# The feed-forward up-projection by one level of Strassen, the gated values by way of DRAM to a down stage of their own

## The chip, the cores and the metric

The kernel runs on one core of a Trainium2 chip. The metric is the device time of one execution in microseconds (us). The five engines of the core are TensorE (PE in the rows, and PEld for its weight loads), VectorE (DVE), ScalarE (ACT), GpSimd (POOL) and SyncE (SP), which issues the DMAs. Each engine works through its own instructions in order; semaphores join them.

## The reference

One layer of a hybrid decoder for 1056 tokens, of which 1024 are a prompt and 32 are samples (8 streams of 4). A state-space and an RWKV mixing sub-layer, an attention to a memory, and a feed-forward sub-layer with a causal convolution follow one another; the change touches the last one alone, and the norm ahead of it:

```python
def rmsnorm(x, g):
    xf = x.astype(jnp.float32)
    y = xf * lax.rsqrt(jnp.mean(xf * xf, axis=-1, keepdims=True) + EPS)
    return (y * g.astype(jnp.float32)).astype(x.dtype)

def conv_ffn(h, buf, w_up, conv_w, conv_b, w_down):
    up = h @ w_up                                   # 1024 -> 2 * 2816
    up, new_buf = causal_dwconv(up, buf, conv_w, conv_b)    # width 3
    gate, val = jnp.split(up, 2, axis=-1)
    return (jax.nn.silu(gate) * val) @ w_down, new_buf

    x = x + cross_attn(rmsnorm(x, p["norm_xa_w"]), mem_k, mem_v, p["xa_w_q"], p["xa_w_o"])
    f, ffn_conv_n = conv_ffn(rmsnorm(x, p["norm_ffn_w"]), ffn_conv, ...)
    return x + f, ...
```

## The kernel before

Everything is laid out with the channels in the 128 partitions and the tokens along the free axis. A product in float32 precision is made of three: each operand is split in a rounded high part and the rest (`split`, L142: a cast on ScalarE, L143, and a subtraction on VectorE, L144), and TensorE adds high by high, high by low and low by high into one PSUM bank. Weights come in tiles of 128 x 1024 by SyncE, are split, and wait in two rings, `w_hi` and `w_lo`. A scheduler sets each engine's order from the order of the code and the rings of buffers, so an instruction can move ahead of others that come before it in the code.

The tokens lie in two halves, 512 and 544 columns (the second holds the samples). `phase_e` is the attention's output projection, once for the half of 544 and then for that of 512: eight tiles m, each 24 matmuls a piece (`gemm`, L217; pieces of 272 + 272 and of 512), the addition of x (L1376, into `pt`, which was loaded at L1374), the split of the sum times the norm's gain into `xq` (L147, L148), the sum of squares (L268, L271), and a store to `x2_d`. The root of the mean square (`row_roots`, L246, L229, L233) and its spreading over the partitions (`spread`, L255) come after all eight tiles. Nobody waits for them there: the root `rbf` is multiplied in later, as `up` evicts its banks (L1464, L1461).

The feed-forward runs over 22 pairs j of projection tiles. `up` makes one tile of 128 channels for all tokens (L1454: pieces of 512, 272 and 272 columns), convolves it (ScalarE L1440 and L1442 for the middle tap, VectorE L1444 and L1446 for the two others), and takes the silu of the first of the pair (L1494). `up_pair` multiplies the two (L1497) and splits the result into `hh`. Groups of 4, 4, 4, 4, 2 and 4 pairs go to `down_all`, which adds their share of the down product into the residual tiles x2 (L1484, L1486; three pieces of 352 columns) while the next group's first pair is made. The last group (L1542) is done in columns of 400, 400 and 256, with the final norm of one piece beside the next. GpSimd has only small work here: a fill of two columns (L1433) and copies of 2 and 16 columns (L1434, L1467, L1468) per tile, and the power of `inv_root` (L233).

## Time and profile before

| what | value |
| --- | --- |
| median of three runs | 1953.26 us (1951.85 to 1959.46) |
| the profiled execution | 1949.68 us |
| its span, first to last instruction | 1947.9 us |
| outside of the span | 1.8 us |
| TensorE busy | 1870.5 us, 96% of the span |
| VectorE busy | 1198.4 us, 62% |
| ScalarE busy | 714.6 us, 37% |
| GpSimd busy | 128.4 us, 7% |

The share of busy time is an average over the stages. A stage is read by its window (who is busy, at which granted clock of TensorE) and by the chain of waits, which follows back from the last instruction what released each step. Up and down take 1181 to 1886 us of the span, the output projection ahead of them some 1080 to 1167, and the last group with the final norm the rest. The profiled execution is 3.6 us shorter than the median.

### The profile page before, as it was taken

The numbers are of one execution on the slowest core, as the hardware profiler recorded it, in microseconds if no ns is written. First come the engines' busy times: TensorE is split into PE (matmuls) and PEld (weight loads), VectorE is DVE, ScalarE is ACT, GpSimd is POOL, SyncE is SP. The second block draws the span as 40 slices with busy tenths as digits, with TensorE's granted clock in tenths as the row PEclk, the third lists the DMA queues.
The fourth block names the chain that finished last, engine by engine and source line by source line (L and its number), as shares of the span: only waits on it lengthen the run. The fifth ranks groups of instructions, "written<-read, shape, count | busy, mean of one in ns | idle before, by whom it ended". The sixth has DMA issues, their size and how long they took to land.

```text
span 1947.9 us, 34518 instructions
## 1 busy us (share of the span) xinstructions
PE 1870.5 (96%) x14150; PEld 1628.5 (84%) x14150; DVE 1198.4 (62%) x2357; ACT 714.6 (37%) x1256; POOL 128.4 (7%) x316
## 2 busy tenths in 40 slices
PE   6999999989999999999999999999999999999997
PEld 6797788865777667799866988999999999999997
DVE  5657677687686677656745645654655545645566
ACT  4443335445444444335534433322322312312231
POOL 0011111010110110000000001000000000000000
PEclk9999999989999899999999999999999999999999
DMA  7521113053222123365266572112112111121112
GB/s 252 174 68 42 37 46 108 30 169 120 79 55 67 53 66 100 120 230 197 82 231 218 157 235 90 43 34 66 33 44 62 32 51 53 31 67 45 44 52 90
DMA packets 104094, 183.78 MB, mean 94 GB/s; under 512 B 36928, under 2 KB 49536, under 8 KB 103936
## 3 DMA queue, kind: packets, MB, share of 16 engines
q1 hardware_dynamic: 103936, 181.58, 30.6%
q8 instruction: 111, 1.82, 0.4%
q14 instruction: 47, 0.39, 0.1%
HBM read 154.32 MB, written 27.22 MB: 93 GB/s over the span
## 4 chain that ended last, share of the span: by engine, by line
PE 81%; DMA 6%; DVE 5%; ACT 3%; POOL 2%; issue 1%; SPq 0%; POOLq 0%; DVEq 0%; ACTq 0%
PE ps_g L217 21%; PE ps_c L1454 10%; PE ps_g L1454 10%; PE ps_y L217 4%; PE ps_g L1484 4%; PE ps_c L1484 4%; PE ps_y L1454 3%; PE ps_x L1454 3%; PE ps_x L1484 2%; PE ps_y L1484 2%; POOL ir_r L233 1%; PE ps_m L535 1%; PE ps_x L608 1%; DVE w_lo L144 1%; DMA dx<-s 1%
## 5 line engine op out<-in xcount | busy, mean ns | idle before, releaser
L217 PE MATMUL ps_g<-act,w_hi 128*128 128x272 f32 (+1 forms) x1728 | 429.8, 336 | 0.2 <-DVE rv L842 0.2
L143 ACT CAST w_hi<-w_raw 128x1024 fp32r<-128x1024 f32 (+1 forms) x196 | 191.8, 979 | 511.4 <-PE ps_g L217 143.6
L217 PEld LDWEIGHTS ps_g<-act,w_hi 128*128 128x128 f32 x1728 | 293.4, 192 | 38.9 <-issue 11.7
L217 PE MATMUL ps_g<-act,w_lo 128*128 128x272 f32 (+1 forms) x864 | 290.6, 336 | 0.1
L144 DVE TENSOR_TENSOR w_lo<-w_raw,w_hi 128x1024 fp32r<-128x1024 f32 (+1 forms) x196 | 222.9, 1137 | 102.3 <-ACT w_hi L143 98.7
L217 PEld LDWEIGHTS ps_g<-act,w_lo 128*128 128x128 f32 x864 | 165.8, 192 | 18.1 <-issue 5.1
L1454 PE MATMUL ps_g<-xq,w_hi 128*128 128x512 f32 (+1 forms) x704 | 177.2, 340 | 0.0
L1454 PE MATMUL ps_c<-xq,w_hi 128*128 128x512 f32 (+1 forms) x704 | 176.9, 340 | 0.0
L1454 PEld LDWEIGHTS ps_g<-xq,w_hi 128*128 128x128 f32 x704 | 121.8, 188 | 14.3
L1454 PEld LDWEIGHTS ps_c<-xq,w_hi 128*128 128x128 f32 x704 | 121.6, 188 | 14.2
L1454 PE MATMUL ps_g<-xq,w_lo 128*128 128x512 f32 (+1 forms) x352 | 119.6, 340 | 0.0
L1454 PE MATMUL ps_c<-xq,w_lo 128*128 128x512 f32 (+1 forms) x352 | 119.5, 340 | 0.0
L1444 DVE SCALAR_TENSOR_TENSOR fo<-fu,vec,fo 128x1024 f32<-128x1024 f32 (+1 forms) x90 | 113.4, 1260 | 6.9 <-ACT fo L1440 5.3
L217 PE MATMUL ps_g<-xq,w_hi 128*128 128x272 f32 (+1 forms) x336 | 85.7, 340 | 0.0
L1454 PEld LDWEIGHTS ps_c<-xq,w_lo 128*128 128x128 f32 x352 | 66.0, 188 | 7.7
L1454 PEld LDWEIGHTS ps_g<-xq,w_lo 128*128 128x128 f32 x352 | 66.0, 188 | 7.6
L1484 PE MATMUL ps_c<-hh,w_hi 128*128 128x352 f32 x288 | 69.7, 323 | 0.0
L1484 PE MATMUL ps_g<-hh,w_hi 128*128 128x352 f32 x288 | 69.7, 323 | 0.0
L1454 PE MATMUL ps_y<-xq,w_hi 128*128 128x272 f32 x352 | 66.4, 286 | 0.0
L1454 PE MATMUL ps_x<-xq,w_hi 128*128 128x272 f32 x352 | 66.4, 286 | 0.0
L1442 ACT ACTIVATE fo<-fus,vec 128x32 f32<-128x32 f32 x44 | 18.2, 414 | 129.0 <-DVE fus L1461 129.0
L217 PEld LDWEIGHTS ps_g<-xq,w_hi 128*128 128x128 f32 x336 | 57.2, 188 | 9.1 <-issue 3.3
(599 smaller groups left out, 3754.9 us busy)
## 6 DMA issues: line engine op xcount, KB each, us to landing
w_raw<-i_w_in SPq DMA_DIRECT2D x52, 512.0 KB, 3.7
w_raw<-i_w_up SPq DMA_DIRECT2D x44, 512.0 KB, 3.7
w_raw<-i_w_out SPq DMA_DIRECT2D x16, 512.0 KB, 4.3
w_raw<-i_xa_w_q SPq DMA_DIRECT2D x16, 512.0 KB, 3.7
ck<-i_ck SPq DMA_DIRECT2D x16, 512.0 KB, 4.5
ck<-i_cv SPq DMA_DIRECT2D x16, 512.0 KB, 4.2
w_raw<-i_xa_w_o SPq DMA_DIRECT2D x16, 512.0 KB, 4.0
w_raw<-i_w_down SPq DMA_DIRECT2D x32, 256.0 KB, 2.7
```

Source lines behind the costliest of these rows:

```text
L143: S.copy(out=hi, in_=src)
L144: V.tensor_tensor(out=lo, in0=src, in1=hi.bitcast(F32), op=ALU.subtract)
L217: PE.matmul(pt[:, :n], a[:, k], b, start=i == 0, stop=i == 3 * nk - 1)
L233: G.tensor_tensor(out=r[:rows, :n], in0=v[:rows, :n], in1=nhalf[:rows, 0:1].to_broadcast([rows, n]), op=ALU.pow)
L535: PE.matmul(pts[e][:, c * P:c * P + P], BK[hs, 4 * q + c, bkw[e]], KQ[hs, 4 * q + c, :], start=True, stop=True)
L608: PE.matmul(py_[hs, c * 64:c * 64 + 64], EE[hs, c, :], Y[hs, c, :], start=True, stop=True)
L1442: S.activation(out=os_, in_=us_[:, :, 2:6], func=AF.Identity, scale=w3[2], bias=vc("fb", mt))
L1444: V.scalar_tensor_tensor(out=o[:, lo:hi], in0=ub[:, j + lo:j + hi], scalar=w3[j], in1=o[:, lo:hi], op0=ALU.mult, op1=ALU.add)
L1454: PE.matmul(pt[:, :n], a[:, k], xf[k][:, b, lo:lo + n], start=i == 0, stop=i == 3 * KT - 1)
L1484: PE.matmul(pt[:, :NW], a[:, k], hs_[k][:, b, cols], start=i == 0, stop=i == 3 * n - 1)
```

## The change

The residual half is kept as it is (`raw`), and the norm is applied before the product. `phase_e` loses the split; a new `operands` scales the half (L1419), cuts it in two along the channels (k and 4 + k) and along the tokens (`lo` and `hi`, 272 or 256 columns each), and makes the seven operands of one Strassen level from the four quarters: B11, T3, T2, T1, T4, B21 and B22, each split in high and low. `up_quads` makes the seven weights of a pair: the weights of the gate tile (`wg`) and of the value tile (`wu`) are the two rows of the left factor, their halves along the input channels its columns. Four of the seven are sums or differences, made by GpSimd (s1 to s4: L1454, L1455, L1457, L1459). `up_pair` runs the seven products, each over 4 k with 272 and 256 columns (L1527), adds them up in eight banks and three helpers (c1 by ScalarE, L1530; u2 and u3 by VectorE, L1532 and L1534), convolves, gates (L1558) and stores the result in DRAM (`h_d`, L1559). When all 22 pairs are done, `hidden` loads them back (L1584) and splits them, and the down product runs as a stage of its own, in four pieces of 264 columns; the last group too.

```diff
-        def phase_e(h, oa, then=lambda m: None):
...
-                xr = pt_()[:, :width]
...
-                a = xp_tile()
-                split_gain(a[:, 0, :width], a[:, 1, :width], xr, vc("nffn", m))
...
+        def phase_e(h, oa):
...
+                xr = rawp.tile([P, width], F32, name=f"raw{h}", bufs=KT)
+                nc.sync.dma_start(out=xr, in_=x1_d[m, :, off:off + width])
...
+            return raw, row_roots([acc], width, one_d, EPS)
+
+        def operands(h, raw, root):
...
+            def scale(k):
+                for pt, lo, w in rs:
+                    V.scalar_tensor_tensor(out=raw[k][:, lo:lo + w], in0=raw[k][:, lo:lo + w], scalar=vc("nffn", k), in1=pt[:, :w], op0=ALU.mult, op1=ALU.mult)
...
+            for k in range(4):
+                scale(4 + k)
+                V.tensor_tensor(out=hi[k], in0=hi[4 + k], in1=hi[k], op=ALU.subtract)
+                put("T3", k, hi[k])
+                V.tensor_tensor(out=lo[k], in0=lo[k], in1=hi[k], op=ALU.add)
+                put("T2", k, lo[k])
+            for k in range(4):
+                V.tensor_tensor(out=hi[k], in0=hi[4 + k], in1=lo[k], op=ALU.subtract)
+                put("T1", k, hi[k])
+                V.tensor_tensor(out=lo[k], in0=lo[4 + k], in1=lo[k], op=ALU.subtract)
+                put("T4", k, lo[k])
...
+        def up_quads():
...
+                wu = f1.tile([P, KT, P], F32, name="w_raw2", bufs=1)
+                nc.sync.dma_start(out=wu, in_=I["w_up"][FT + j])
+                s1, s2, s3, s4 = (f1.tile([P, 4, P], F32, name="ws", bufs=3) for _ in range(4))
+                for q in range(7):
+                    if q == 1:
+                        G.tensor_tensor(out=s1, in0=wu[:, 0:4], in1=wu[:, 4:8], op=ALU.add)
+                        G.tensor_tensor(out=s2, in0=s1, in1=wg[:, 0:4], op=ALU.subtract)
+                    if q == 2:
+                        G.tensor_tensor(out=s3, in0=wg[:, 0:4], in1=wu[:, 0:4], op=ALU.subtract)
+                    if q == 6:
+                        G.tensor_tensor(out=s4, in0=wg[:, 4:8], in1=s2, op=ALU.subtract)
+                    x = (wg[:, 0:4], s2, s3, wu[:, 4:8], s1, wg[:, 4:8], s4)[q]
...
+            for step_, (name, bank, more) in enumerate((("B11", 0, False), ("T2", 1, False), ("T3", 2, False), ("T4", 2, True), ("T1", 3, False), ("B21", 0, True), ("B22", 3, True))):
+                w = next(quads)
+                for q, X in ((1, X1), (0, X0)):
...
+                    if step_ == 0:
+                        S.copy(out=c1[q], in_=pt[:, :n])
+                    elif step_ == 1:
+                        V.tensor_tensor(out=u2[q], in0=c1[q], in1=pt[:, :n], op=ALU.add)
+                    elif step_ == 2:
+                        V.tensor_tensor(out=u3[q], in0=u2[q], in1=pt[:, :n], op=ALU.add)
+                    elif step_ == 3:
+                        out(1, 0, q, add(u2[q], pt))
...
+            nc.sync.dma_start(out=h_d[j], in_=os_[1])
...
+        def hidden(j):
+
+            o = ff.tile([P, NTOK], F32, name="fo", bufs=4)
+            nc.sync.dma_start(out=o, in_=h_d[j])
```

Three places where the order of instructions moves. The first is VectorE at the border between the two halves of `phase_e`. Before, the last tile's eviction, split and squares stand directly ahead of the first eviction (L1376) and the weight splits of the half of 512:

```order
L1376 TENSOR_TENSOR pt_11974<-pt_11974,ps_g_12007 128x272
L144 TENSOR_TENSOR w_lo_12061<-w_raw_12058,w_hi_12060 128x1024
L148 SCALAR_TENSOR_TENSOR xq_12034<-pt_11974,vec_85,xq_12034 128x544
L271 TENSOR_TENSOR acc_11499<-acc_11499,pt_12037 128x544
L229 TENSOR_SCALAR ir_v_12051<-ps_c_12042 68x8
L1376 TENSOR_TENSOR pt_12056<-pt_12056,ps_y_12064 128x512
L144 TENSOR_TENSOR w_lo_12112<-w_raw_12109,w_hi_12111 128x1024
```

Now (`raw1` and `raw0` are the residual tiles of the halves of 544 and 512, `act` and `xq` hold operands), the 60 instructions of `operands` for the half of 544 stand there, of which these are the last ones:

```order
L144 TENSOR_TENSOR act_12054<-raw1_11769,act_12054 128x272
L144 TENSOR_TENSOR act_12054<-raw1_11834,act_12054 128x272
L144 TENSOR_TENSOR act_12055<-raw1_11899,act_12055 128x272
L144 TENSOR_TENSOR act_12055<-raw1_11964,act_12055 128x272
L1397 TENSOR_TENSOR raw0_12155<-raw0_12155,ps_y_12163 128x512
L144 TENSOR_TENSOR w_lo_12196<-w_raw_12193,w_hi_12195 128x1024
```

The eviction and the weight split have moved behind the whole of `operands`. The same holds at the border to the first pair, with 52 instructions.

The second is VectorE around the end of a pair in the up stage. Before, at a pair's end with a group's down product beside it:

```order
L1464 TENSOR_TENSOR fu_14533<-ps_x_14591,rbf_8712 128x272
L144 TENSOR_TENSOR w_lo_14631<-w_raw_14628,w_hi_14630 128x512
L1444 SCALAR_TENSOR_TENSOR fo_14537<-fu_14533,vec_85,fo_14537 128x1024
L1486 TENSOR_TENSOR act_12409<-ps_g_14634,act_12409 128x352
L1444 SCALAR_TENSOR_TENSOR fo_14537<-fu_14533,vec_85,fo_14537 128x1024
L1486 TENSOR_TENSOR act_12409<-ps_g_14648,act_12409 128x352
L1497 TENSOR_TENSOR fo_14537<-fo_14537,fo_14438 128x1056
```

Now, from the last product's eviction of one pair to u3 of the next (`w_hi` and `w_lo` are the targets of weight splits):

```order
L1512 TENSOR_TENSOR fu_14928<-u20_14946,ps_m_14942 128x256
L144 TENSOR_TENSOR w_hi_15138<-ws_15074,w_hi_15138 128x512
L1551 SCALAR_TENSOR_TENSOR fo_15167<-fu_14928,vec_85,fo_15167 128x1024
L1551 SCALAR_TENSOR_TENSOR fo_15177<-fu_14929,vec_85,fo_15177 128x1024
L1551 SCALAR_TENSOR_TENSOR fo_15167<-fu_14928,vec_85,fo_15167 128x1024
L1552 SCALAR_TENSOR_TENSOR fo_15177<-fus_14931,vec_85,fo_15177 128x32
L1551 SCALAR_TENSOR_TENSOR fo_15177<-fu_14929,vec_85,fo_15177 128x1024
L1552 SCALAR_TENSOR_TENSOR fo_15177<-fus_14931,vec_85,fo_15177 128x32
L144 TENSOR_TENSOR w_hi_15239<-ws_15072,w_hi_15239 128x512
L1558 TENSOR_TENSOR fo_15177<-fo_15177,fo_15167 128x1056
L1532 TENSOR_TENSOR u21_15207<-c11_15205,ps_c_15199 128x272
L1532 TENSOR_TENSOR u20_15206<-c10_15204,ps_y_15198 128x256
```

All four taps and the gating now stand together, between the evictions of a pair's last product and the sums u2, and u3 of the next pair (two rows further) stands behind them.

The third is GpSimd at the same place. Before, it has only fills and copies of a few columns:

```order
L1468 COPY fs_12426<-fus_14435 128x16
L1434 COPY fus_15020<-sst_12427 128x8x2
L1467 COPY fp_12425<-fu_14434 128x2
L1433 MEMSET fu_15019 128x2
L1468 COPY fs_12426<-fus_14534 128x16
```

Now the weight sums stand among them (L1459 is s4 of one pair, L1454, L1455 and L1457 are s1, s2 and s3 of the next):

```order
L1553 COPY fp_12564<-fu_14668 128x2
L1459 TENSOR_TENSOR ws_14815<-w_raw_14808,ws_14813 128x512
L1454 TENSOR_TENSOR ws_15072<-w_raw2_15070 128x512
L1491 MEMSET fu_14928 128x2
L1491 MEMSET fu_14929 128x2
L1492 COPY fus_14931<-sst_12566 128x8x2
L1455 TENSOR_TENSOR ws_15073<-ws_15072,w_raw_15068 128x512
L1457 TENSOR_TENSOR ws_15074<-w_raw_15068,w_raw2_15070 128x512
```

s4 and the next pair's s1 stand one behind the other, ahead of the fills that wait for the taps.

## Rows read from the trace of the kernel before

**Rows 1.** Windows: stretch, length, busy us (count) PE PEld DVE ACT POOL, clock, DMA share, GB/s.

```profile
1168.00:1181.00 13.00, 12.20 (x80) 11.00 (x80) 6.88 (x12) 3.64 (x7) 1.34 (x4) 1.00 0.62 201
1181.00:1886.00 705.00, 705.00 (x4392) 662.32 (x4391) 392.50 (x588) 185.33 (x210) 30.60 (x172) 1.00 0.16 47
```

**Rows 2.** The chain of waits in the up and down stage: start, duration in us, what.

```profile
1325.81 3.88 PE ps_c L1484 x24
1343.16 8.53 PE ps_c L1454 x48
1351.69 2.99 PE ps_x L1454 x24
```

**Rows 3.** The chain of waits near the end, the last group's 256 columns.

```profile
1924.85 1.43 PE ps_x L1542 x12
```

**Rows 4.** The chain of waits at the output projection and the first up tile.

```profile
1079.14 3.05 PE ps_m L1287 x12
1121.26 3.69 PE ps_y L217 x16
1128.77 11.05 PE ps_g L217 x48
1139.82 5.49 PE ps_y L217 x24
1167.29 4.81 PE ps_g L1454 x21
```

**Rows 5.** DMA issues: destination and source, queue, count, size, us to landing.

```profile
act<-x_d SPq DMA_DIRECT2D x8, 528.0 KB, 4.7
x_d<-pt SPq DMA_DIRECT2D x16, 256.0 KB, 2.2
pt<-x_d SPq DMA_DIRECT2D x8, 272.0 KB, 2.9
```

**Rows 6.** Groups by form on DVE: form and count, busy us, mean ns, idle before.

```profile
L1444 DVE SCALAR_TENSOR_TENSOR fo<-fu,vec,fo 128x1024 f32<-128x1024 f32 x86 | 110.4, 1284 | 6.4 <-ACT fo L1440 4.7 <-issue 0.3
L1497 DVE TENSOR_TENSOR fo<-fo 128x1056 f32<-128x1056 f32 x21 | 26.4, 1257 | 0.6
L144 DVE TENSOR_TENSOR w_lo<-w_raw,w_hi 128x512 fp32r<-128x512 f32 x32 | 22.3, 696 | 0.7
L148 DVE SCALAR_TENSOR_TENSOR xq<-pt,vec,xq 128x512 fp32r<-128x512 f32 x16 | 11.4, 747 | 1.1 <-ACT xq L147 1.1
L1464 DVE TENSOR_TENSOR fu<-ps_y,rbf 128x272 f32<-128x272 f32 x22 | 9.7, 442 | 37.0 <-PE ps_y L1454 37.0
```

**Rows 7.** The timeline of DVE: start, us, what; two instructions merged in one row.

```profile
689.73 1.29 DVE L537 TENSOR_TENSOR W<-ps_m,cst 128x512 f32<-128x512 f32 x2 [0.26 <-PE ps_m L535]
```

**Rows 8.** The windows around an early gap of TensorE, columns as in rows 1.

```profile
425.00:431.00 6.00, 0.47 (x1) 0.18 (x1) 5.71 (x19) 2.51 (x7) 0.31 (x1) 0.50 0.59 149
431.00:434.00 3.00, 2.68 (x8) 0.97 (x8) 2.31 (x9) 0.84 (x2) 0.00 (x0) 0.50 0.96 313
```

**Rows 9.** Groups by form on ACT.

```profile
L143 ACT CAST w_hi<-w_raw 128x512 fp32r<-128x512 f32 x32 | 19.9, 621 | 132.6 <-PE ps_x L1484 58.0 <-PE ps_y L1484 57.4 <-PE ps_x L1454 8.6
L1440 ACT ACTIVATE fo<-fu,vec 128x1024 f32<-128x1024 f32 x43 | 53.5, 1244 | 0.0
```

**Rows 10.** The timeline at one tap, and two GpSimd lines' durations (min/median/max in ns).

```profile
1185.02 1.28 DVE L1444 SCALAR_TENSOR_TENSOR fo<-fu,vec,fo 128x1024 f32<-128x1024 f32 x1
1185.26 1.10 POOL L1434 COPY fus<-sst 128x16 f32<-128x16 f32 x1 [2.75 <-DVE fo L1446]
...
L1434 POOL COPY fus<-sst x44: 197/198/1097, 1182.2 to 1862.0; 128x16 f32<-128x16 f32 x44
...
L447 POOL COPY last_u<-ub x28: 178/752/1757, 82.4 to 696.0; 128x1 f32<-128x1 f32 x28
```

**Rows 11.** Groups by form on POOL.

```profile
L474 POOL MEMSET Mt<- 128x1024 f32 x1 | 1.0, 951 | 0.0
L1057 POOL COPY hp<-xcs 128x192 f32<-128x192 f32 x1 | 0.6, 603 | 5.8 <-PE ps_m L785 5.8
```

More of the change, by code (lines that the diff above doesn't have):

```diff
@@ L1471, in hybrid_step @@
-        LAST = ((0, 400), (400, 400), (800, 256))
-        NP = 3
-        NW = NTOK // NP
+        NW = NTOK // 4
+        LAST = tuple((i * NW, NW) for i in range(4))
+        def hidden(j):
+            o = ff.tile([P, NTOK], F32, name="fo", bufs=4)
+            nc.sync.dma_start(out=o, in_=h_d[j])
+            hh = [xp_tile()[:, :, :2 * NW] for _ in range(2)]
+            for i in range(2):
+                split(hh[i][:, 0], hh[i][:, 1], o[:, 2 * NW * i:2 * NW * i + 2 * NW])
+            return hh
```

252 lines of the change are left out of this document (146 added, 106 removed).

## The prediction

> **What bounds the kernel now.** I read the windows first, stage by stage, then the chain of waits for the length of each product, then the groups by form for what stands on the other engines. From 1181 to 1886 us, where up and down alternate, TensorE is busy in all 705 us, at the full granted clock (2.4 GHz); VectorE has 392.5 us of work there and GpSimd 30.6 [rows 1]. No wait ends last in that stage: it is as long as its matmuls, so a multiplication that is left out is worth its whole time there, as long as its operands still come in time. So the prediction has two halves, what the matmuls give back and where TensorE now has to wait.
>
> **What the matmuls give back.** One projection tile is 24 matmuls of 512 and 24 of 272 columns, 8.53 us, and 24 more of 272, 2.99 us [rows 2]: 11.52 us, 44 times, 506.9 us. After, a pair of tiles is seven products, each of 12 matmuls of 272 columns (2.99 / 24 = 124.6 ns) and 12 of 256 (1.43 / 12 = 119.2 ns, [rows 3]): 7 × 12 × 243.8 ns = 20.48 us, 22 times, 450.5 us. That is **−56.4 us**. The down products keep their columns and are cut in four pieces of 264 where there were three of 352. A 352 costs 3.88 / 24 = 161.7 ns [rows 2]; for a 264 I take 122 ns, between the two short ones: 1728 × 122 − 1296 × 161.7 = +1.2 us, and the last group the same way less than that; together I book **+1.1 us**.
>
> **The hand-over into the output projection, +3.7 us.** The residual tiles have a new place in SBUF, over buffers that the last head's matmuls read. Before, x was prefetched while softmax still ran; now its load waits for the matmuls of L1287, which begin at 1079.14 and end by 1082.2 [rows 4]. A load of 272 KB lands after 2.9 us [rows 5], two additions of 0.44 us follow [rows 6], and only then are the banks free: about 1085.9, where TensorE went on at 1082.2.
>
> **Between the two halves of the output projection, +19.5 us.** Normalizing and building the seven operand sets is new on VectorE: per half 28 splits and 16 sums, and scalings on top (16 for the half of 544 columns, 8 for the other). In the order these stand in one piece ahead of the first eviction of the second half and ahead of the split of its third weight tile. Two subtractions of 512 back to back take 1.29 us where one alone takes 0.70, so each gives 0.10 us to the one before [rows 7]. A sum of 272 is then 0.442 − 0.10 = 0.35 us [rows 6], and a scaling, by the 0.05 that it costs more at 512 [rows 6], 0.40: 44 × 0.35 + 16 × 0.40 = 21.8 us. Count from T1 = 1121.26, where the first half's products end [rows 4]. The scale is spread 7.5 us later (1128.77), the operands are done at 29.3, an eviction (0.6) and a weight split (1.2) bring TensorE its next tile at T1+31.1. TensorE meanwhile has two weight tiles ready: the first ends with the roots at T1+7.5, the second (5.49 us, [rows 4]) at 13.0. It is idle for 18 us, and the six tiles that are left end at 31.1 + 6 × 5.49 = 64.0, where before the stage ended at 1167.29, T1+46.0: +18.0. After a gap the clock has to come back: around 431 us TensorE sat nearly idle for 6 us, and the 3 us of matmuls after it still ran at the granted clock of 0.50, which is 1.2 GHz [rows 8]. 3 us at half speed lose 1.5 us: **+19.5 us**.
>
> **Before the first pair, +16.5 us.** The same again for the half of 512. Evicting, squaring, root and spreading took at most 7.5 us above; six are enough here. Then 8 scalings of 512 at 0.65 and 44 of 256 at 0.34: 20.2 us. At T2+27 the first weight that stands behind them is split. TensorE has by then done the products on the half of 544 columns and waits with 90 of 168 matmuls to go, 11 us: pair 0 ends at T2+38.7, not at 20.5, **+18.2**. The stall that stood at the same place before falls away: 0.8 us of 13 idle [rows 1] and some 1.4 us of root matmuls that now lie in the gap, −2.2; a cold clock takes 0 to 1.5 again. I book **+16.5**.
>
> **From up to down, +11.7 us.** The hidden values come back from DRAM. The x2 loads wait for the last products (their tiles were operands), and the first two loads of hidden values stand behind them on SyncE. One of 528 KB lands after 4.7 us [rows 5], a split follows, so TensorE begins some 6.3 us late and works for 4.4 us on the two it has; the third and fourth load stand behind the store of the last pair, which comes 9 us after the last product (below), and the fourth also waits for it to land, 2.2 us by a store of 256 KB [rows 5]: 9 + 2.2 + 4.7 + 0.6 = 16.5. Of that 4.4 + 2.2 us are work: 10 us idle, with the clock **+11.7**. The bound above is 17, if the eight x2 loads in flight slow the others.
>
> **Without anything more** the sum is −56.4 + 1.1 + 3.7 + 19.5 + 16.5 + 11.7 = −3.9 us: 1945.8 against the profiled execution of 1949.68. That execution lies 3.6 us under the median of 1953.26; against the median it is 1949.4.
>
> **Inside the stage: who holds whom.** Per pair VectorE now has some 14.7 us of work in 20.5, but in one lump. Let t = 0 be the end of a pair's last product. Its eviction ends at 0.5, a cast (0.62) and the first tap (1.24) on ScalarE [rows 9] at 2.0; four taps of 1.28 less the overlap, 1.2 each [rows 6], with the sample columns end at 7.2, a weight split (0.6) at 7.8, the gating (1.26 less the overlap, [rows 6]) at 9.0, two sums u2 at 9.7, a split at 10.3, and u3 at 10.65. The product T4 adds into the bank from which u3 reads, so TensorE waits for it. It gets there after six and a bit of the short products: 3 × 2.93 for B11, T2, T3, half of T1 (1.50) and three matmuls, 10.65. There is no slack: what delays VectorE in these 10 us is a stall, 21 times.
>
> GpSimd now makes four weight sums of 512 columns per pair. A GpSimd copy of 16 elements that began under a tap of VectorE took 1.10 us and ended 0.06 us after the tap; the same copy takes 0.20 us as a rule, and one of a single element runs from 178 to 1757 ns [rows 10]. With two inputs in SBUF, VectorE holds GpSimd off. That GpSimd holds VectorE off as long, no row shows: its pieces in before are too short. I take it that it does, since whatever keeps the second out is held by the first. The Trainium skill, "SBUF — State Buffer", section "Who interferes with whom", says the same and more: VectorE with two SBUF inputs and a GpSimd instruction that reads SBUF take the same port pair, whoever comes first has it for the whole instruction, the other is fully blocked. By that rule each sum that gets in costs its whole length; were the lock on GpSimd's side alone, the sum would stay at 1949.
>
> What a sum of 512 takes is bounded by a fill of 1024, 951 ns, so 0.5 us, and by a copy of 192 in 603 ns, so 1.6 [rows 11]; 192 columns there were partly blocked, so I take the middle, 1.0. (The Trainium skill, "GPSIMD Engine Reference", section 3.1, has 4497 ns for an addition of 2048, an estimate of 1.12 here; with it the stall would be 1.7 us a pair instead of 1.5.) The order puts s4 at t = 1.45, released by a split: it ends at 2.45 and the taps begin 0.4 late. s1 of the next pair follows as its load lands, within the taps: 1.0. s2 is released at the split before the gating and mostly runs under the u2 sums, whose input is in PSUM: 0.1. s3 lies later. **1.5 us a pair, 21 times, +31.5 us**; with 0.5 per sum it is 0.5 a pair (+10), with 1.6 it is 2.6 (+55).
>
> **Forecast:** 1945.8 + 31.5 = 1977.3 against the profiled execution, 3.6 more against the median: **1981 us**.
>
> **The rivals.** *GpSimd doesn't stop VectorE* (not slower): its sums fall in the gaps of VectorE, or only GpSimd is held off, as the rows of before literally show. Then 1949, no change. It decides at 0.65 us of stall a pair; below that the time is under 1963. For it: VectorE has 6 us free in each pair. Against: they lie after t = 11, and three of the four sums are released before. *The hand-overs overlap* (faster): if the order of the operands lets TensorE begin the first pair's early products while the later operands are made, and ScalarE's casts hide, half of 19.5 + 16.5 + 11.7 goes, with no stall in the pairs: 1949 − 24 = 1925. Against: the rows of VectorE's order stand in one lump, and a queue runs in order. *The heavy end*: 2.6 a pair, 2004.
>
> **How the numbers follow.** About 0.5%, 10 us, is what a measurement of this kernel can tell from no change, so the bounds are 1943 and 1963. The forecast with its heavy end has 0.58. No stall, or one under 0.65 a pair, 0.27; the hand-overs cheap, 0.15. The range runs from 1941 (no stall, hand-overs 8 us cheaper) to 2004 and leaves out most of the faster case and a little above.
>
> **What would show it.** Right: 20.5 us of matmuls but a pair every 22; TensorE's wait ahead of T4 ended by VectorE's u3; taps of over 1.28 us where a GpSimd sum runs; gaps of 18, 16 and 10 us at the three hand-overs. Wrong: a pair every 20.5 us, taps at their old 1.28; or gaps under 8 us; or GpSimd itself late, with TensorE waiting for a weight split.

## The result: 2.4% slower

The changed kernel takes 2002.51 us (median, 1994.44 to 2003.99), the kernel before 1952.55 us in the same comparison: a ratio of 1.0244, with a 95% interval of 1.0203 to 1.0285. The forecast was 1981 us, slower, with a range of 1941 to 2004; its direction and mechanism came in, and the sum was 21.5 us short.

The profiled execution of the changed kernel took 2003.78 us, with a span of 2002.0 us. Its page begins with the busy times, and its fourth part sums the chain that ended last:

```profile
PE 1846.5 (92%) x15248; PEld 1632.6 (82%) x15248; DVE 1338.2 (67%) x2711; ACT 790.5 (39%) x1541; POOL 287.9 (14%) x405
...
PE 67%; DVE 13%; issue 7%; ACT 5%; DMA 5%; POOL 2%; SPq 0%; POOLq 0%; ACTq 0%; DVEq 0%
```

TensorE's busy time fell by 24 us (1870.5 before), and not by the 56 us that a matmul count gives. In part that is because matmuls that run at a lower granted clock are busy for longer; in part it stands in the pairs, at the full clock: the 21 pairs behind the first are busy for 442.87 us, where the count gives 430.1. The idle time of TensorE doubled, from 77 to 156 us. The windows show where; the first is one pair of the up stage, from just behind the last product of one pair to just behind that of the next, then come four around the passage between the two halves of the output projection (the root, the matmuls after it, the gap, the matmuls after that), the middle of the first pair and the whole of it, the other 21 pairs, and the start of the down products. Columns are as in [rows 1]: length, then busy us (and instructions) of PE, PEld, DVE, ACT and POOL, the granted clock, the DMA share and GB/s.

```profile
1279.37:1302.40 23.03, 21.10 (x170) 20.68 (x169) 17.49 (x28) 9.33 (x17) 8.72 (x12) 1.00 0.21 71
1126.00:1128.00 2.00, 0.24 (x3) 0.01 (x1) 0.00 (x0) 0.00 (x0) 1.64 (x1) 1.00 0.26 100
1130.00:1133.00 3.00, 3.00 (x9) 2.32 (x8) 2.32 (x7) 1.83 (x4) 0.00 (x0) 0.51 0.01 3
1138.00:1154.00 16.00, 0.50 (x3) 0.10 (x1) 14.79 (x41) 9.37 (x25) 0.00 (x0) 0.66 0.00 0
1154.00:1163.00 9.00, 9.00 (x26) 6.78 (x27) 3.47 (x5) 1.48 (x3) 0.00 (x0) 0.65 0.53 177
1197.00:1221.00 24.00, 14.92 (x64) 11.45 (x62) 22.95 (x57) 11.64 (x32) 2.09 (x4) 0.73 0.06 15
1190.28:1233.10 42.82, 31.62 (x182) 27.71 (x182) 32.38 (x75) 16.45 (x43) 8.86 (x14) 0.80 0.13 42
1233.10:1715.21 482.11, 442.87 (x3528) 433.96 (x3527) 364.76 (x565) 196.01 (x356) 176.90 (x248) 1.00 0.21 75
1724.00:1730.00 6.00, 5.82 (x26) 5.79 (x27) 2.64 (x4) 1.83 (x4) 0.00 (x0) 0.50 0.92 294
```

Against [rows 1], where TensorE was busy in every microsecond of the stage, a pair now has 1.93 us in which it stands still. In the 16 us of the gap VectorE works on the operands almost without a break, and TensorE has three matmuls; in the next line TensorE is busy throughout, but at a mean granted clock of 0.65 (0.50 is its lower level, 1.2 GHz). The same stands on a smaller scale at the root: 1.76 us in which TensorE waits, and then 3 us of matmuls at 0.51. In the kernel before, the root passed at the same distance from the first half's end without this:

```profile
1126.00:1128.00 2.00, 2.00 (x9) 1.32 (x8) 0.16 (x1) 0.15 (x1) 1.60 (x1) 1.00 0.55 211
1130.00:1133.00 3.00, 3.00 (x14) 2.44 (x14) 0.16 (x1) 0.00 (x0) 0.00 (x0) 1.00 0.60 202
```

(windows of the kernel before, columns as above; its first half ends within 0.3 us of the same time).

The timeline of TensorE names the waits (start, us, what; in brackets the idle time before and what ended it). The first of these is the hand-over into the output projection, the second the one between its halves, the third is in the first pair, the fourth in an ordinary pair, the last the hand-over to the down products:

```profile
1080.65 0.52 PE L214 MATMUL ps_g<-act,w_hi 128*128 128x272 f32 x2 [3.48 <-DVE raw L1397]
...
1153.93 1.19 PE L214 MATMUL ps_y<-xq,w_hi 128*128 128x512 f32 x2 [15.50 <-DVE raw L1397]
...
1218.90 1.96 PE L1527 MATMUL ps_m<-act,w_hi 128*128 128x272 f32 x7 [3.38 <-DVE w_hi L144]
...
1292.14 1.77 PE L1527 MATMUL ps_x<-xq,w_lo 128*128 128x272 f32 x12 [1.49 <-DVE u L1534]
...
1724.18 0.81 PE L1603 MATMUL ps_g<-xq,w_hi 128*128 128x264 f32 x2 [8.97 <-ACT xq L143]
```

The fourth is the product T4, which waits for VectorE's u3 (L1534), as the prediction had it. It returns with 1.48 to 1.49 us in 19 pairs, and over the whole stage it comes to 30.8 us:

```profile
L1527 PE MATMUL ps_x<-xq,w_lo 128*128 128x272 f32 x264 | 40.3, 303 | 30.8 <-DVE u L1534 30.8
```

Why u3 is late stands on VectorE and GpSimd in that same pair, VectorE's rows first:

```profile
1281.17 5.43 DVE L1551 SCALAR_TENSOR_TENSOR fo<-fu,vec,fo 128x1024 f32<-128x1024 f32 x3 [0.46 <-ACT fo L1548]
...
1286.69 1.27 DVE L1551 SCALAR_TENSOR_TENSOR fo<-fu,vec,fo 128x1024 f32<-128x1024 f32 x1
...
1289.82 0.42 DVE L1532 TENSOR_TENSOR u<-c,ps_c 128x272 f32<-128x272 f32 x1
1290.17 0.41 DVE L1532 TENSOR_TENSOR u<-c,ps_y 128x256 f32<-128x256 f32 x1
1290.50 1.24 DVE L144 TENSOR_TENSOR w_lo<-w_raw,w_lo 128x512 fp32r<-128x512 f32 x1
1291.67 0.42 DVE L1534 TENSOR_TENSOR u<-u,ps_x 128x272 f32<-128x272 f32 x1
...
1280.80 1.29 POOL L1459 TENSOR_TENSOR ws<-w_raw,ws 128x512 f32<-128x512 f32 x1 [2.20 <-DVE w_hi L144]
1282.17 2.16 POOL L1454 TENSOR_TENSOR ws<-w_raw 128x512 f32<-128x512 f32 x1
...
1288.26 1.70 POOL L1492 COPY fus<-sst 128x16 f32<-128x16 f32 x1
1289.92 1.28 POOL L1455 TENSOR_TENSOR ws<-ws,w_raw 128x512 f32<-128x512 f32 x1
```

The sum s4 (L1459) begins 0.37 us ahead of the first tap and ends 0.92 us after the tap's start. s1 (L1454) stands waiting from 1282.17, gets in between two taps, and ends at 1284.33; alone such a sum takes 1.29. The three taps that are merged in the first row end 5.43 us after they began; without GpSimd beside them three take 3.68 us (experiments 1, 4 and 9). A fourth tap without company takes 1.27. s2 (L1455) begins at 1289.92 beside the two u2 sums, which have one input in PSUM and keep their 0.42 us, and then meets the weight split at 1290.50, which has two inputs in SBUF and takes 1.24 instead of 0.69. So 1.75 us and some 0.55 us stand ahead of u3. s2 comes at that place because a copy of 16 columns (L1492) stands ahead of it in GpSimd's order: alone it takes 0.20 us, but here it begins in a split, lasts through the gating (L1558, from 1288.65 to 1289.90) and ends at 1289.96.

Over all pairs, the tap's group (88 instructions, mean 1683 ns) stands against 1284 ns in [rows 6]; s1, which waits among them, stands with 2061 ns:

```profile
L1551 DVE SCALAR_TENSOR_TENSOR fo<-fu,vec,fo 128x1024 f32<-128x1024 f32 x88 | 144.8, 1683 | 10.1 <-ACT fo L1548 10.1
L1454 POOL TENSOR_TENSOR ws<-w_raw 128x512 f32<-128x512 f32 x22 | 45.3, 2061 | 158.0 <-ACT xq L143 156.0 <-DMA w_raw<-i_w_up 0.4
```

**The balance of the two profiled executions**, stage by stage, from where TensorE's stages end (spans of 2002.0 and 1947.9 us):

| stage | after − before, matmul saving set apart | predicted |
| --- | --- | --- |
| all ahead of the output projection (not touched) | −5.0 | 0 |
| first half of the output projection | +5.3 | +3.7 |
| second half, with the gap ahead of it | +22.8 | +19.5 |
| first pair | +20.0 | +16.5 |
| the other 21 pairs, over 20.48 us each | +52.0 | +31.5 |
| down products and final norm | +15.5 | +12.8 |
| up matmuls, by the count | −56.4 | −56.4 |
| sum | +54.2 | +27.6 |

### The profile page after: what moved, and what is told of

The parts are those of the page before. It is cut to its first block, busy times and chain, and to the rows that moved or that the text cites. A ratio compares the mean times of both kernels' runs of the same rounds, so it can differ in the third digit from the quotient of the medians.

```text
span 2002.0 us, 37716 instructions
## 1 busy us (share of the span) xinstructions
PE 1846.5 (92%) x15248; PEld 1632.6 (82%) x15248; DVE 1338.2 (67%) x2711; ACT 790.5 (39%) x1541; POOL 287.9 (14%) x405
## 3 DMA queue, kind: packets, MB, share of 16 engines
q1 hardware_dynamic: 111424, 205.37, 31.5%
## 4 chain that ended last, share of the span: by engine, by line
PE 67%; DVE 13%; issue 7%; ACT 5%; DMA 5%; POOL 2%; SPq 0%; POOLq 0%; ACTq 0%; DVEq 0%
PE ps_g L214 21%; PE ps_m L1527 4%; PE ps_y L214 4%; DVE fo L1551 4%; PE ps_g L1603 3%; PE ps_c L1603 3%; PE ps_g L1527 3%; PE ps_x L1527 2%; PE ps_y L1603 2%; PE ps_c L1527 2%; PE ps_x L1603 2%; ACT fo L1548 1%; POOL ir_r L230 1%; DVE fo L1558 1%; ACT w_hi L143 1%
## 5 line engine op out<-in xcount | busy, mean ns | idle before, releaser
L144 DVE TENSOR_TENSOR w_lo<-w_raw,w_hi 128x1024 fp32r<-128x1024 f32 (+1 forms) x152 | 168.9, 1111 | 77.9 <-ACT w_hi L143 72.5
L1551 DVE SCALAR_TENSOR_TENSOR fo<-fu,vec,fo 128x1024 f32<-128x1024 f32 x88 | 144.8, 1683 | 10.1 <-ACT fo L1548 10.1
L1527 PE MATMUL ps_m<-act,w_hi 128*128 128x272 f32 x528 | 79.9, 294 | 13.2 <-DVE w_hi L144 12.1
L1527 PEld LDWEIGHTS ps_m<-act,w_hi 128*128 128x128 f32 x528 | 70.3, 190 | 18.1 <-DVE w_hi L144 16.9
L1603 PE MATMUL ps_g<-xq,w_hi 128*128 128x264 f32 x392 | 74.5, 287 | 9.0 <-ACT xq L143 9.0
L1527 PE MATMUL ps_m<-xq,w_hi 128*128 128x256 f32 x528 | 74.2, 283 | 0.0
L1527 PE MATMUL ps_c<-xq,w_lo 128*128 128x272 f32 (+1 forms) x528 | 72.4, 286 | 0.0
L1603 PE MATMUL ps_c<-xq,w_hi 128*128 128x264 f32 x380 | 71.9, 286 | 0.0
L1603 PEld LDWEIGHTS ps_g<-xq,w_hi 128*128 128x128 f32 x392 | 61.9, 191 | 9.2 <-ACT xq L143 9.2
L1527 PE MATMUL ps_x<-xq,w_lo 128*128 128x272 f32 x264 | 40.3, 303 | 30.8 <-DVE u L1534 30.8
L1527 PEld LDWEIGHTS ps_m<-xq,w_hi 128*128 128x128 f32 x528 | 68.3, 191 | 0.0
L1527 PEld LDWEIGHTS ps_c<-xq,w_lo 128*128 128x128 f32 x528 | 68.2, 191 | 0.0
L1454 POOL TENSOR_TENSOR ws<-w_raw 128x512 f32<-128x512 f32 x22 | 45.3, 2061 | 158.0 <-ACT xq L143 156.0
L214 PEld LDWEIGHTS ps_g<-xq,w_hi 128*128 128x128 f32 x336 | 59.2, 194 | 10.1 <-issue 3.3
```

The lines of the kernel that those rows point to most:

```text
L144: V.tensor_tensor(out=lo, in0=src, in1=hi.bitcast(F32), op=ALU.subtract)
L214: PE.matmul(pt[:, :n], a[:, k], b, start=i == 0, stop=i == 3 * nk - 1)
L1454: G.tensor_tensor(out=s1, in0=wu[:, 0:4], in1=wu[:, 4:8], op=ALU.add)
L1527: PE.matmul(pt[:, :n], w[:, a], X[name][k][:, b], start=i == 0 and not more, stop=i == 11, skip_group_check=True)
L1551: V.scalar_tensor_tensor(out=o[:, 0:2 * T], in0=ub[i][:, t:t + 2 * T], scalar=w3[t], in1=o[:, 0:2 * T], op0=ALU.mult, op1=ALU.add)
L1603: PE.matmul(pt[:, :NW], a[:, k], x[:, b], start=i == 0, stop=i == 3 * n - 1)
```

## The experiments

The theory to be tested: what makes a pair longer is GpSimd's *reading* of SBUF during VectorE's taps and splits, and u3 has no slack, so that each delay goes into the time whole. The rival: the pair is longer for another reason (VectorE's larger load as such, the order of the products, the loads), and the stretched taps only go along with it.

**1. Without the four weight sums.** The products get the unsummed weight halves in their place, so four of seven products are not those of the reference; all else stays.

```diff
-                        G.tensor_tensor(out=s1, in0=wu[:, 0:4], in1=wu[:, 4:8], op=ALU.add)
-                        G.tensor_tensor(out=s2, in0=s1, in1=wg[:, 0:4], op=ALU.subtract)
...
-                        G.tensor_tensor(out=s3, in0=wg[:, 0:4], in1=wu[:, 0:4], op=ALU.subtract)
...
-                        G.tensor_tensor(out=s4, in0=wg[:, 4:8], in1=s2, op=ALU.subtract)
```

> GpSimd's four weight sums of a pair are left out (the products take the unsummed weights in their place, so the output is not the reference's); all else stands. In the changed kernel a pair takes 23.03 us, of which 7 x 2.94 = 20.6 are products. If GpSimd's sums hold VectorE's two-input instructions off (the lock), the taps go back to 1.28 us, u3 comes in time, no gap stands ahead of T4 and a pair takes 20.6 us: 21 x 2.45 = 51 us less, about 1951 us. If VectorE's lump of work is too late by itself, or the weight splits are, the gap of 1.49 us stays in most part and a pair takes over 22 us: 1980 or more.

Measured: 1951.19 us, ratio to before 1.0005 [0.9971, 1.0038]. The groups of VectorE's taps and of TensorE's first T4 product:

```profile
L1543 DVE SCALAR_TENSOR_TENSOR fo<-fu,vec,fo 128x1024 f32<-128x1024 f32 x88 | 109.0, 1280 | 12.0 <-ACT fo L1540 12.0
...
L1519 PE MATMUL ps_x<-xq,w_lo 128*128 128x272 f32 x264 | 39.4, 299 | 0.4 <-DVE u L1526 0.4
```

The taps have their old 1280 ns, and TensorE's wait for u3 has gone from 30.8 us in all to 0.4. A pair takes 20.72 us. So the sums cost 2.31 us a pair (23.03 − 20.72), and some 50 us in all, as much as the whole loss. This shows that they are the cause, not yet how.

**2. The sums on VectorE.** The same four sums, 0.69 us each there, `V` for `G`:

```diff
-                        G.tensor_tensor(out=s1, in0=wu[:, 0:4], in1=wu[:, 4:8], op=ALU.add)
+                        V.tensor_tensor(out=s1, in0=wu[:, 0:4], in1=wu[:, 4:8], op=ALU.add)
```

> The same four sums, on VectorE in place of GpSimd. VectorE gets 4 x 0.6 = 2.4 us more a pair (some 17 of 20.6), s4 ahead of the taps, where it fits into the wait for ScalarE, and the three others behind u3. By the lock nothing but the work itself is left: taps of 1.28 us, u3 at most 0.2 us late, a pair of 20.6 to 21.0 us, 1951 to 1960 us. If the amount of work on VectorE were the cause, this is the worst place for the sums: over 23 us a pair, 2002 or more.

Measured: 1952.55 us, ratio 1.0016 [0.9996, 1.0036]; a pair takes 20.71 to 20.72 us, a tap 1278 ns:

```profile
L1551 DVE SCALAR_TENSOR_TENSOR fo<-fu,vec,fo 128x1024 f32<-128x1024 f32 x88 | 108.9, 1278 | 0.5 <-ACT fo L1548 0.5
```

VectorE does more work than in the changed kernel, and the pair is as short as without the sums. VectorE's load as such is therefore not what makes the pair long, and the rival loses its first form.

**3. The operands of the first half queued behind the evictions of the second.** `operands` is cut into 20 steps, and some of them are placed behind the eviction of each tile of the second half, so that TensorE's banks come free sooner:

```diff
+        def some(m, ev):
+            with tc.issue_after(ev.ins):
+                for _ in range((3, 3, 3, 3, 2, 2, 2, 2)[m]):
+                    next(ops1, None)
+        raw0, root0 = phase_e(0, oa0, some)
```

> Only the operands of the half of 544 columns move: VectorE's 60 instructions are queued two or three steps behind each eviction of the half of 512, not in one piece ahead of the first. If that lump is what makes TensorE idle for 15.5 us at the border and lets the clock fall behind it, the second half of the output projection ends some 48 us after the first, not 68.8: 20 us less, about 1982 us. If VectorE has no room for it there (2.6 us of own work and some 2.7 of operands in a tile of 5.49 us), tiles are stretched and under 10 us are won.

Measured: 1993.21 us, ratio 1.0219 [1.018, 1.0258]. Against the changed kernel this is 9 us, where 20 were expected. In the trace the gap of 15.50 us is gone, and two smaller ones stand at the third tile, one of 0.94 us and this one:

```profile
1151.86 0.53 PE L214 MATMUL ps_g<-xq,w_lo 128*128 128x512 f32 x1 [2.87 <-DVE w_lo L144]
```

The second half of the output projection ends at 1175.15 instead of 1190.28 us, with all ahead of it 0.4 us later: 15.6 us gained there, some 5 fewer than expected. Three steps ahead of the third tile's weight split were too many; the split (L144) had to wait for them. The rest of the shortfall in the median does not show in this trace, which is 15.1 us shorter than that of the changed kernel (1988.69 against 2003.78); two of the four executions took 1998 us and left no trace. A pair still takes 23.03 us. So the gap between the halves was a matter of order, as the prediction said, and a cost of its own beside the pairs.

**4. The same sums on GpSimd, but later.** A GpSimd copy of one column that reads u3 stands ahead of s4, and s1 to s3 follow it; so the four sums run after u3, and not beside the taps.

```diff
+                        with (tc.issue_after(behind[-1]) if behind else ExitStack()):
+                            G.tensor_tensor(out=s1, in0=wu[:, 0:4], in1=wu[:, 4:8], op=ALU.add)
...
+                        tk = f1.tile([P, 1], F32, name="tk", bufs=2)
+                        t_ = G.tensor_copy(out=tk, in_=u3s[-1][:, 0:1])
+                        with tc.issue_after(t_.ins):
+                            behind.append(G.tensor_tensor(out=s4, in0=wg[:, 4:8], in1=s2, op=ALU.subtract).ins)
```

> The four sums stay on GpSimd with all their work, and are only held back: s4 of a pair and with it s1, s2 and s3 of the next wait for u3 of that pair, so they run while VectorE has gaps. By the lock the taps are 1.28 us again, u3 is in time, and a pair takes 20.6 to 21 us: 1951 to 1960 us, as with no sums at all. If the sums cost by their work or by bandwidth, wherever they stand, nothing is won; if the weights are now late, TensorE waits for a weight split ahead of B22 or of the next pair's T2 instead.

Measured: 1953.37 us, ratio 0.9999 [0.9958, 1.004]. From the timeline, VectorE's taps of one pair and the split behind u3, then GpSimd's first two sums of that pair:

```profile
1294.12 3.68 DVE L1558 SCALAR_TENSOR_TENSOR fo<-fu,vec,fo 128x1024 f32<-128x1024 f32 x3 [0.45 <-ACT fo L1555]
...
1305.25 1.11 DVE L144 TENSOR_TENSOR w_hi<-ws,w_hi 128x512 fp32r<-128x512 f32 x1 [1.85 <-ACT w_hi L143]
...
1303.25 1.31 POOL L1465 TENSOR_TENSOR ws<-w_raw,ws 128x512 f32<-128x512 f32 x1
1304.52 1.30 POOL L1457 TENSOR_TENSOR ws<-w_raw 128x512 f32<-128x512 f32 x1
```

Nothing is left out, no sum is shorter, and a pair takes 20.71 us. The sums still hold VectorE off: the split at 1305.25 takes 1.11 instead of 0.69 us. But there no product waits for VectorE. So it is the place of the sums that costs, and a collision of the same kind costs nothing 10 us later.

**5. All together.** Late sums, the interleaved operands with a lighter start (2, 2, 1, 1, 1, 1, 2, 2), and the first three hidden values loaded in tiles of their own while the last pairs still run:

```diff
+                for _ in range((2, 2, 1, 1, 1, 1, 2, 2)[m]):
+                    next(ops1, None)
...
+            if j == FT - 3:
+                for i in range(3):
+                    o = ff.tile([P, NTOK], F32, name="fh", bufs=3)
+                    nc.sync.dma_start(out=o, in_=h_d[i])
+                    first.append(o)
```

> Three edits together: the late sums, the operands of the half of 544 queued behind the evictions of the half of 512 (with a more even share per tile than the first try, whose third tile waited 3.8 us), and the hidden values of the first three pairs loaded back during the up stage. Late sums alone gave 1953 us. The border should give 18 us (15.5 by the trace of the first try, and most of its 3.8), the border to down 7 of its 8.4: 1953 - 25 = 1928 us, 1.1% under the kernel before. If the borders' gaps only move on to the next wait (the roots, the first pair's operands, the loads of x2), 1940 or more.

Measured: 1930.12 us, ratio 0.9927 [0.9901, 0.9952]: faster than before, as expected. TensorE's up stage is again without a hole, seven products for eight:

```profile
1240.00:1600.00 360.00, 360.00 (x2921) 358.43 (x2921) 275.78 (x473) 158.89 (x296) 160.45 (x224) 1.00 0.22 81
```

The second half of the output projection ends at 1169.7 us and the gap to the down products is 2.76 us, where 8.97 stood. A new wait stands at the border to the first pair. VectorE works on the leftover operands of the half of 544 columns (first row, six splits in one), while GpSimd's power for the root waits beside them and with it TensorE's spreading of the scale:

```profile
1175.81 2.19 DVE L144 TENSOR_TENSOR act<-raw,act 128x272 fp32r<-128x272 f32 x6
...
1174.91 3.96 POOL L230 TENSOR_TENSOR ir_r<-ir_v,nhalf 128x4 f32<-128x4 f32 x1 [12.10 <-DVE ir_v L226]
...
1178.93 1.12 PE L252 MATMUL ps_c<-ident,ir_r 128*128 128x128 f32 x4 [4.47 <-POOL ir_r L230]
```

**6. Fills in place of the sums.** Each sum is replaced by two GpSimd fills, one of the sum's tile (512 elements) and one of a scratch tile (904), which only write; the products are not those of the reference.

```diff
-                        G.tensor_tensor(out=s1, in0=wu[:, 0:4], in1=wu[:, 4:8], op=ALU.add)
-                        G.tensor_tensor(out=s2, in0=s1, in1=wg[:, 0:4], op=ALU.subtract)
+                        G.memset(s1[:, 0:4], 0.25); G.memset(scr, 0.0)
+                        G.memset(s2[:, 0:4], 0.25); G.memset(scr, 0.0)
```

> In place of each of GpSimd's sums stand two fills, of 512 and 904 columns, which only write, and take about as long (some 1.3 us); the weights are wrong by that, so the output is not the reference's. If the lock is on what GpSimd reads, as the Trainium skill says (SBUF - State Buffer, Who interferes with whom), the taps are 1.28 us, a pair is 20.7 and the time 1951. If any GpSimd work of that length there stops VectorE, the taps stay near 1.7 us, a pair is over 22 and the time 1985 or more.

Measured: 1950.1 us, ratio 1.0008 [0.999, 1.0025]; a tap takes 1280 ns. That would speak for the theory, but the trace takes the verdict away: the 88 scratch fills depend on nothing, and the scheduler placed them ahead of the stage, from 1076 to 1158 us. In the pairs only the short fills stood:

```profile
1079.34 0.85 POOL L1460 MEMSET scr<- 128x904 f32 x1
...
1281.47 0.53 POOL L1458 MEMSET ws<- 128x512 f32 x1 [2.10 <-DVE w_hi L144]
```

0.53 us for 1.28 is no equal burden. Inconclusive, and repeated in experiment 9.

**7. s1 twice.** One more sum among the taps:

```diff
+                        G.tensor_tensor(out=s1, in0=wu[:, 0:4], in1=wu[:, 4:8], op=ALU.add)
```

> GpSimd makes s1 twice, one right after the other, all else as in the changed kernel. If each sum that gets in costs VectorE its whole length, the second gets in at the next border between two taps and costs 1.2 us more a pair, 21 times: 26 us, about 2028. If what is lost is a fixed wait per pair (one turn of the lock), 2002 stays.

Measured: 2022.62 us, ratio 1.0395 [1.0357, 1.0432], 20 us over the changed kernel where 26 were expected. The taps and the two sums of one pair:

```profile
1282.60 6.47 DVE L1552 SCALAR_TENSOR_TENSOR fo<-fu,vec,fo 128x1024 f32<-128x1024 f32 x3 [0.45 <-ACT fo L1549]
...
1283.60 2.16 POOL L1454 TENSOR_TENSOR ws<-w_raw 128x512 f32<-128x512 f32 x1
1285.83 2.15 POOL L1455 TENSOR_TENSOR ws<-w_raw 128x512 f32<-128x512 f32 x1
```

The three taps take 6.47 instead of 5.43 us, and a pair 24.07 instead of 23.03: 1.04 us in both. What the taps lose goes into the pair one for one, which is the second half of the theory. The sum itself costs less than its length of 1.28 us (the expectation took 1.2); the traces don't show where the rest goes.

The changed kernel holds a smaller dose as well. At the taps ahead of its last pair s4 stands alone, since no further pair needs an s1 and an s2:

```profile
1695.68 4.39 DVE L1551 SCALAR_TENSOR_TENSOR fo<-fu,vec,fo 128x1024 f32<-128x1024 f32 x3 [0.45 <-ACT fo L1548]
...
1695.31 1.29 POOL L1459 TENSOR_TENSOR ws<-w_raw,ws 128x512 f32<-128x512 f32 x1 [2.20 <-DVE w_hi L144]
```

The split ahead of u3 keeps its 0.68 us there, and the last pair takes 21.42 us, 0.70 over a pair without sums (20.72). With none, one, two and three sums beside them, three taps thus take 3.68, 4.39, 5.43 and 6.47 us: s4 costs 0.71, and each sum that waits and gets in 1.04.

**8. Late sums and the early loads of hidden values**, without the interleaving: the edits of experiment 4 and the last piece of the diff of experiment 5.

> The late sums, and the hidden values of the first three pairs loaded back during the up stage into tiles of their own. If the gap of 7.7 us at the border to down is the wait for these loads and for the last pair's store, it shrinks to 1 or 2 us: 6 to 7 less than the late sums alone, about 1946. If the x2 loads or the splits end it, it stays above 5.

Measured: 1943.64 us, ratio 0.9974 [0.9951, 0.9998]. The gap ahead of the down products is 1.27 us:

```profile
1674.19 0.51 PE L1617 MATMUL ps_g<-xq,w_hi 128*128 128x264 f32 x2 [1.27 <-ACT xq L143]
```

Against experiment 4, where this gap was 7.74 us, that is 9.7 us less: 6.5 of gap, and most of the rest is what the clock lost there behind it (a granted clock of 0.56 over the first 6 us of down products there, which is 2.6 us, and of 1.00 here). Against experiment 5 it leaves 13.5 us for the interleaving, where the trace of experiment 3 had 15.6.

**9. Long fills, held in place.** As experiment 6, but the scratch fill is placed right behind the fill of the sum's tile, so that both stand where the sum stood:

```diff
+            def fill(t):
+                with tc.issue_after(G.memset(t, 0.25).ins):
+                    G.memset(ff.tile([P, 904], F32, name="scr", bufs=1), 0.0)
...
+                        fill(s1)
+                        fill(s2)
```

> In the run before, the longer of the two fills was moved out of the up stage by the scheduler, so only fills of 0.53 us stood there. Now each of GpSimd's sums is a fill of 512 columns with one of 904 held right behind it, some 1.4 us, so that the first tap, and the split behind the gating, run beside a fill; the weights are wrong by that, so the output is not the reference's. If only what GpSimd reads collides with VectorE's two-input instructions (the Trainium skill, SBUF - State Buffer, Who interferes with whom), the taps stay at 1.28 us, a pair at 20.7 and the time at about 1950. If fills hold VectorE off as well, the taps come to 1.5 us or more on average, a pair to over 21.5 and the time to 1970 or more.

Measured: 1951.44 us, ratio 0.9996 [0.996, 1.0033]; a pair takes 20.71 us. One pair's fills and VectorE's taps, and the tap's group:

```profile
1283.40 0.53 POOL L1448 MEMSET ws<- 128x512 f32 x1 [2.18 <-DVE w_hi L144]
1283.87 0.85 POOL L1449 MEMSET scr<- 128x904 f32 x1
...
1283.80 3.68 DVE L1555 SCALAR_TENSOR_TENSOR fo<-fu,vec,fo 128x1024 f32<-128x1024 f32 x3 [0.45 <-ACT fo L1552]
```

```profile
L1555 DVE SCALAR_TENSOR_TENSOR fo<-fu,vec,fo 128x1024 f32<-128x1024 f32 x88 | 109.1, 1281 | 10.0 <-ACT fo L1552 10.0
```

GpSimd is at work for about as long as one sum, and the first tap runs beside it from 1283.80 to the end of the fill at 1284.72. Those 0.92 us are as long as the first tap ran beside s4 in the changed kernel, where it cost 0.71 us; here no tap is longer. The fills in place of s2 stand beside the split ahead of u3, which keeps its 0.68 us; the others lie later. So it is not GpSimd's being busy that stops VectorE; what a sum does and a fill doesn't is to read SBUF (and to add, see below). The Trainium skill, "SBUF — State Buffer", section "Who interferes with whom", says just this: a VectorE instruction with two SBUF inputs contends with a GpSimd instruction that reads SBUF, and not with one that only writes. Runs 1, 4 and 9 agree with it, and so does the u2 sum, with one input in PSUM, that kept its 0.42 us beside s2.

**10. Experiment 5 with the leftover operands later.** The last steps of the half of 544 columns (T1 and T4 in part, B21, B22) are queued behind the first operands of the half of 512, so that VectorE is free when the root is due:

```diff
+                for _ in range((2, 2, 1, 1, 1, 1, 2, 0)[m]):
...
+        ops0 = operands(0, raw0, root0)
+        for _ in range(8):
+            t2 = next(ops0)
+        with tc.issue_after(t2.ins):
+            for _ in ops1:
+                pass
+        for _ in ops0:
+            pass
```

> The three edits together, and what was left of the operands of the half of 544 (its last T1 and T4, and B21 and B22, which the first pair needs last) moved behind the first operands of the half of 512. In the three edits the power on GpSimd took 3.96 us and not 1.03, beside a row of splits on VectorE that stood there. If that was the lock, on the chain to the first pair, it takes 1.03 again and the first pair is ready about 3 us earlier: 1927 us against 1930. If the operands as a whole set the first pair's end, whatever their order, the power is short again and the time stays.

Measured: 1928.66 us, ratio 0.9863 [0.981, 0.9915]. The power takes 1.02 us again, and TensorE's spreading comes 4.4 us earlier than in experiment 5 (2.9 us, counted from the end of the first half); but the gap has moved to a weight split behind the operands, which comes as late as it did:

```profile
1173.42 1.02 POOL L230 TENSOR_TENSOR ir_r<-ir_v,nhalf 128x4 f32<-128x4 f32 x1 [12.08 <-DVE ir_v L226]
...
1174.49 1.11 PE L252 MATMUL ps_c<-ident,ir_r 128*128 128x128 f32 x4 [0.99 <-POOL ir_r L230]
...
1202.05 2.63 PE L1553 MATMUL ps_m<-act,w_hi 128*128 128x272 f32 x10 [3.04 <-DVE w_hi L144]
```

The profiled executions, 1928.99 us here and 1930.63 in experiment 5, are 1.6 us apart, less than the scatter of one kernel; counted from the end of the attention's last product they took 850.9 and 850.0 us. The wait for the power was a real one, but what ends last there is VectorE's row of operands. Both versions beat both kernels, by 0.7 to 1.4% of the time before; between the two nothing is settled.

## Why the prediction was right, and where its sum was short

**The matmuls.** 7 for 8 gave what the count said, but for a little: 24 short matmuls took 2.94 to 2.96 us instead of 2.925, and a pair without waits 20.72 instead of 20.48, 5 us in all 22. The net without the sums was thus rightly put near zero: −3.9 us predicted, and experiments 1, 2, 4 and 9, which have the hand-overs but not the lock, all lie within 0.2% of before. The traces are finer: counted from the end of the attention's last product on, without the part that isn't touched, these four take 871.8 to 873.8 us where the kernel before takes 865.7. So the net was +6 to +8 us and not −3.9, by the longer products and the hand-overs (below); the medians scatter too much to show it.

**"GpSimd holds VectorE off as long."** Right, and it was the step that no row before showed. The rows of before had only the other direction ([rows 10]). Both directions stand in the pair shown above, and experiment 9 ties them to the reads.

**"There is no slack."** Right: u3 comes 2.31 us later after a pair's last eviction than without the sums in its way (12.35 against 10.04 us), and the pair is 2.31 us longer; experiment 7 adds 1.04 to both. Of the 2.31, 1.93 is idle time; in the rest TensorE is counted as busy, 21.10 instead of 20.72 us. Most of that rest is the two waits of a pair: a matmul of 272 columns stands in the trace with 0.29 us, of which 0.12 count where the next one follows at once, and all of them ahead of a wait (an estimate: twice 0.17 us).

**The step that failed** is the size of the lock: 1.5 us a pair predicted, 2.31 measured, 21 times 0.8. Two of its three terms were short. A sum of 512 was taken as 1.0 us, in the middle between a fill (0.5) and a partly blocked copy (1.6), and takes 1.28: s4, which begins ahead of the first tap, reached further into it and cost 0.71 us, not 0.4. s1 cost 1.04 and was booked at 1.0, which is luck in part, since its length was wrong as well. The figure of the Trainium skill, "GPSIMD Engine Reference", section 3.1, scaled down to an estimate of 1.12, was nearer than 1.0, and short too. And s2 was booked at 0.1, because it should run beside u2, whose input is in PSUM; it did, but it was not over when the split ahead of u3 came, and that split took 0.55 us more. The term counted the neighbour at the start of s2 and not the one at its end. s2 stood there because the copy ahead of it had waited for the gating, which no term held. Twenty pairs at 2.31 us, the last one at 0.7 and the longer products (5 us) make the +52.0 against +31.5.

**The hand-overs.** Three of the gaps came about as forecast, 3.48, 15.50 and 8.97 us against 3.7, 18 and 10. The one in the first pair, forecast as a single wait of 11 us (16 in the list of signs), came as 11.2 us in many pieces, the longest of 3.38. Yet each hand-over cost more, 5.3, 22.8, 20.0 and 15.5 against 3.7, 19.5, 16.5 and 12.8. What was short there is mostly the clock. After 3.48 us of idle time the next 24 matmuls took 4.79 us instead of 2.99, where nothing was booked. Counted from the end of the first half, TensorE was to resume 31.1 us later and did so after 32.4; the six tiles that were left were to take 32.9 us, and 1.5 more for the clock, and took 36.4. The clock lost some 3 us there (9 us at 0.65), and some 1.5 more at the root (3 us at 0.51), where no term stood. The latter didn't set the end, since the operands did; with the wait of 1.76 us it made the gap begin later, 16.9 us after the first half's end instead of 13.0, and so be shorter, 15.50 us instead of 18. The first pair came to 20.0 against 16.5, with a clock of 0.73 over 24 us. At the down products 6 us at 0.50 lost 3 us where 1.7 were booked; with the gap and a second one of 0.63 us that is 12.6 of the 15.5. The pieces of 264 columns took 122 ns, as booked; the rest lies in the tail behind them and wasn't taken apart.

**What offset it.** The untouched part ahead of 1080 us was 5.0 us shorter in the profile after than in that before. This part varies from execution to execution: the 25 executions of the kernel before that stand beside experiments 1 to 4 lie from 1945.84 to 1971.32 us, and in the profiled execution of experiment 4, 1973.13 us, the excess over its median is there, with the attention's last product at 1096 us instead of 1074. Up to there TensorE's instructions are the same and in the same order in all these kernels; that product ends at 1082.2 us in the trace of before, and between 1067.0 and 1099.1 in the 11 traces of the kernels after the change. So the 5.0 us lie well within the scatter, and that they hid a part of the shortfall is luck. Whether the same scatter made experiment 3's median 6 us worse than its trace is not shown.

**The rivals.** "GpSimd doesn't stop VectorE" was priced at 1949 and is refuted as a mechanism; experiment 9, where its fills indeed don't, gives 1951.44. "The hand-overs overlap" did not happen by itself, since VectorE made the operands in one piece (14.79 of the 16 us in the gap); made to happen by code in experiment 5 it gave 1930, near the 1925 that stood there. "The heavy end" was nearest in time (2004), but not by its own terms: the lock came to 2.31 us a pair and not to 2.6, and the hand-overs, which it left as forecast, added the rest.

**What stays open.** Why the power of experiment 5 waited 3.96 us through a row of VectorE splits, and the copy of 16 columns 1.70 us through a split and the gating, where s1 got in between two taps, isn't settled: the traces show all three, and no run changed the spacing of VectorE's instructions alone. That it is the reading which stops VectorE rests on sums and fills, which differ in the addition too; a GpSimd copy as long as a sum, which reads and doesn't add, was not run. That the lower clock is what a hand-over costs beyond its gap is shown at the down products, by experiments 4 and 8; in the first pair it is only read from the window, since no run took its waits away.

## What to carry to other kernels

When work is moved to GpSimd to unburden VectorE, look at what it reads: here a GpSimd sum of 1.28 us cost the VectorE instructions with two SBUF inputs beside it from 0.55 to 1.04 us, and the place decides whether that is paid; the same four sums cost 50 us beside the taps and nothing some 10 us later. A saving in matmuls is worth its count only where operands and hand-overs keep up; here 56 us of matmuls were eaten by four hand-overs and 2.3 us in each pair, and a better order, with three loads made earlier (experiment 5), gave back enough to win. Price a collision by both neighbours of the intruder, the one at its start and the one at its end.

## What the runs showed of the hardware that was not expected

- An addition of two 128 × 512 float32 tiles on GpSimd took 1.27 to 1.32 us, where a fill of the same tile took 0.53 and one of 904 elements 0.85; when it had to wait for a tap it was recorded as 2.16.
- GpSimd's waiting sum got in between two of VectorE's queued taps in each of the 20 pairs in which it stood there (s1, mostly 2.15 to 2.16 us), but a copy of 16 columns beside a split and the gating took 1.70 us instead of 0.20, and a power of 4 columns beside a row of VectorE splits of 272 columns 3.96 us instead of 1.02. A fill just ahead of that copy took 0.10 us.
- VectorE instructions that read one operand from PSUM (u2, 0.42 us) kept their time beside a GpSimd sum; splits with two SBUF inputs went from 0.69 to between 1.11 and 1.24.
- A wait of TensorE of 1.76 us, with 16 matmuls of one column shortly ahead of it and eight of 68 columns right behind it, was followed by 3 busy us at a granted clock of 0.51, one of 3.48 us by 24 matmuls in 4.79 us, one of 8.97 us by 6 us at 0.50, and one of 15.50 us by 9 us at 0.65. The waits of 1.49 us in each pair left the granted clock at 1.00.
